# A hybrid decoder trunk on one core: the swap of the rotary halves by transfers inside SBUF in place of copies on ACT

## The chip, the cores and the metric

The kernel runs on one core of a Trainium2 chip. A core has engines that work side by side, each through its own instructions in order: TensorE (PE, matrix products, with its weight loads shown as PEld), VectorE (DVE), ScalarE (ACT), GpSimd (POOL) and SyncE (SP, which here only issues transfers). The transfers are carried by 16 DMA engines. SBUF is the working memory, 128 partitions wide; PSUM has eight banks that take PE's results. The metric is the device time of one execution, in microseconds (us); lower is better.

## The reference

Two layers over 512 tokens of width 1024, all in float32. Each layer adds three sub-layers to x, each between two RMS norms: a mixer, a gated MLP with a causal convolution of width 3, and a gated embedding. The mixer projects once (`z = h @ w_in`) and splits the columns among three kinds of heads: spatial gating, retention (6 heads of 64) and forgetting attention, FoX (6 heads of 64). The change touches only the rotary step ahead of retention:

```
def rotary(t, positions):
    half = t.shape[-1] // 2
    inv_freq = ROPE_BASE ** (-jnp.arange(half, dtype=jnp.float32) / half)
    ang = positions.astype(jnp.float32)[..., None] * inv_freq
    cos = jnp.cos(ang)[:, :, None, :]
    sin = jnp.sin(ang)[:, :, None, :]
    t1, t2 = t[..., :half], t[..., half:]
    return jnp.concatenate([t1 * cos - t2 * sin, t1 * sin + t2 * cos], axis=-1)
...
        rq = rotary(r_q.astype(jnp.float32).reshape(B, S, N_HEADS_RET, HEAD_DIM), positions)
        rk = rotary(r_k.astype(jnp.float32).reshape(B, S, N_HEADS_RET, HEAD_DIM), positions) * (HEAD_DIM ** -0.5)
        rv = r_v.astype(jnp.float32).reshape(B, S, N_HEADS_RET, HEAD_DIM)
        ro = retention_chunkwise(rq, rk, rv)
```

## The kernel before

**Layout.** Queries and keys of retention are held feature-major: a tile `rm` has 128 partitions, two heads of 64 features, and 512 columns, the tokens. Features 0 to 31 of a head are the first half of the rotary pair, 32 to 63 the second, so swapping the halves moves rows of data between partitions: 32 to 0, 0 to 32, 96 to 64 and 64 to 96.

**The projection.** Weights come in float32 and are split into a high and a low part (a cast on ACT, a subtraction on DVE), so that three faster matmuls make one product. `seven` (L869) computes two 128-row projections, gs and us, at once from seven products instead of eight, in the PSUM banks `beta`, `alpha` and `gamma`; its weights (`graw`, then `wg`, `wu`, `wsa`, `wsb`) need sums that two accumulating transfers from POOL and two adds on DVE make. Its first output is complete with DVE's last add to it, its second with a scaled copy on ACT after the last product, `beta<-hh,wu`.

**The rotary step.** `ret_proj(p)` (L1133) calls `seven` for the query and the key of a pair of heads, then for each of the two matrices `m` takes a scratch tile `rr`, fills it with the swapped halves, and on DVE multiplies m by the cosines in place, rr by the sines, and adds. The in-place product overwrites what the swap reads, so it waits for the swap. `rotary_tables` (L617) makes the two tables once, from positions times the constant `invf`. `ret_core(p)` (L1146) then computes retention for the pair: `ips` are the products of keys and queries, `inn` the decayed scores, `kps` and `kt` the transposed keys, `kvps` and `R` the state, `rops` the outputs, `ro` and `og` their norm and gate, `cc` the concatenation.

**The order of the mixer** is a string of steps (L494):

```
STEPS = "u F H f0 g f1 r0 a0 v a1 G L s r1 r2 c0 f2 c1 c2 a2"
```

f0 to f2 project FoX pairs, a0 to a2 are their attention (`sps` scores, `pe` probabilities, `tps` their transposes, copied to `fet`, then `ops`), r0 to r2 are `ret_proj`, c0 to c2 `ret_core`, v and s belong to retention values and spatial gating, G to the gate. After the mixer come the output projection (weights `traw` to `thl`, products `wo` and `ps`), and the gated MLP in 32 blocks.

**What sets the order on the engines.** The body doesn't issue instructions; it records them. `Plan.record` (L170) notes which recorded operations an operation depends on, by the regions that it reads and writes. `Plan.issue` (L252) then deals the operations out: it steps a clock, keeps for each engine the operations whose inputs are ready and whose buffers can be had, takes the first of them in program order, and advances by a table of costs (L209; a transfer issued by SP costs 525 ns there, then waits for the earlier bytes and 2600 ns more). What comes out is a fixed order for each engine, which the engine follows on the chip, waiting at an instruction whose inputs aren't there. SP's order is made in the same way, so a transfer that waits for its source holds back the transfers behind it on SP. Most small tiles, `rm` and `rr` among them, come from one pool of 12 (L565). An operation that takes another engine or another duration can thus move any operation after it.

Since all operations are recorded through a helper, every row of the trace has line 452; rows are told apart by the names of their tiles.

Of the kernel before, what the change touches and what calls it, by code (L numbers as in the profile page):

```python
# [36 lines left out]
P = 128  # L37
# [433 lines left out]
def constants():  # L471
    idx = np.arange(P, dtype=np.float64)
    lg = np.log(1.0 - 2.0 ** (-5.0 - np.arange(6, dtype=np.float64)))
    diff = idx[None, :] - idx[:, None]
    decay = np.where(diff >= 0, np.exp(lg[:, None, None] * np.maximum(diff, 0.0)), 0.0) / 8.0
    qdec = np.exp(lg[:, None] * (idx + 1.0))
    kdec = np.exp(lg[:, None] * (P - 1.0 - idx)) / 8.0
    cd = np.exp(lg * P)
    hf = np.repeat(np.arange(2), 64)
    c = {}  # L480
    c["ident"] = np.eye(P)
    c["decay"] = decay.transpose(1, 0, 2).reshape(P, 6 * P)
    c["qdec"] = np.stack([qdec[2 * p + hf] for p in range(3)], 1).reshape(P, 3 * P)
    c["kdec"] = kdec.T
    c["cd"] = np.stack([cd[2 * p + hf] for p in range(3)], 1)
    c["invf"] = (10000.0 ** (-np.arange(32, dtype=np.float64) / 32))[np.arange(P) % 32][:, None]
    c["cum"] = np.concatenate([(idx[:, None] <= idx[None, :]).astype(np.float64), np.ones((P, P))], 1)
    c["mask"] = np.where(idx[None, :] <= idx[:, None], 0.0, 1e30)
    return {k: np.ascontiguousarray(v.astype(np.float32)) for k, v in c.items()}
# [51 lines left out]
def body(ctx, tc, a, out):  # L541
    nc = tc.nc
    plan = Plan(tc)
    V, A, G, T, SY = (plan.engine(n, e) for n, e in (
        ("DVE", nc.vector), ("ACT", nc.scalar), ("POOL", nc.gpsimd), ("PE", nc.tensor), ("SP", nc.sync)))
# [19 lines left out]
    def wk(name, shape=(P, 512), dt=F32):  # L565
        return kpt(list(shape), dt, tag="wk", name=name, bufs=12)
# [279 lines left out]
    def seven_weights(src, dma=SUMS_BY_DMA):  # L846

        raw = b8("graw", (2048,))
        load(raw, src.rearrange("p s n -> p (s n)"))
        u2, u1, g1, g2 = (raw[:, i * 512:i * 512 + 512] for i in range(4))  # L850
        wg = b8("wg", (2, 1024), F32R)
        split(wg[:, 0, :], wg[:, 1, :], raw[:, 1024:2048])
        wu = [wk("wu", dt=F32R) for _ in range(2)]
        split(wu[0], wu[1], u2)
        if dma:
            G.dma_start(out=u1, in_=src[:, 0, :], accum_op=ALU.add)
            G.dma_start(out=g1, in_=src[:, 1, :], accum_op=ALU.add)
        else:
            for t, by in ((g1, u1), (u1, u2)):
                V.tensor_tensor(out=t, in0=t, in1=by, op=ALU.add)  # L860
        for t, by in ((u2, g1), (g2, u2)):
            V.tensor_tensor(out=t, in0=t, in1=by, op=ALU.add)
        sa = b8("wsa", (2, 1024), F32R)
        split(sa[:, 0, :], sa[:, 1, :], raw[:, 0:1024])
        sb = b8("wsb", (2, 1024), F32R)
        split(sb[:, 0, :], sb[:, 1, :], raw[:, 1024:2048])
        return wg, wu, sa, sb

    def seven(h, ws, gs, us, scale=1.0, between=None):  # L869

        wg, wu, sa, sb = ws
        be, al, ga = (bank(n)[:, 0:256] for n in ("beta", "alpha", "gamma"))
        t1, t2 = slice(0, 256), slice(256, 512)

        def product(ps, w, n, first, last, part=range(4)):
            for k in part:
                ks = slice(k * P, k * P + P)
                mm3(ps, lambda i: w[i][:, ks], lambda i: h.part(n, i, k), first and k == 0, last and k == 3, True)

        def part(t, i):  # L880
            return [t[:, j, i * 512:i * 512 + 512] for j in range(2)]
        product(be, part(wg, 0), "b11", True, False)
        vbe, val, vga = (in_order(t) for t in (be, al, ga))
        g1, g2, u1, u2 = (halves(t[:, ts]) for t in (gs, us) for ts in (t1, t2))
        A.copy(g1, vbe)
        product(al, part(wg, 1), "b21", True, True)
        V.tensor_tensor(out=g1, in0=val, in1=g1, op=ALU.add)
        product(be, part(sa, 0), "h6", False, False)
        A.copy(g2, vbe)
        product(ga, part(sa, 1), "hd", True, False)  # L890
        if scale == 1.0:
            A.copy(u2, vga)
        else:
            A.mul(u2, vga, -scale)
        product(be, part(sb, 0), "h7", False, False)
        V.scalar_tensor_tensor(out=u2, in0=vbe, scalar=-scale, in1=u2, op0=ALU.mult, op1=ALU.subtract if scale == 1.0 else ALU.add)
        product(ga, part(sb, 1), "b22", False, True)
        V.tensor_tensor(out=g2, in0=vga, in1=g2, op=ALU.add)
        rest = between() if between else None
        product(be, wu, "h4", False, True, range(1) if rest else range(4))  # L900
        if rest:
            rest()
            product(be, wu, "h4", False, True, range(1, 4))
        A.mul(u1, vbe, -scale)
# [60 lines left out]
    def mixers(l, hT, uv, ready):  # L965
# [167 lines left out]
        def ret_proj(p):  # L1133
            res = [wk("rm") for _ in range(2)]
            seven(hT, seven_weights(a["w_fm"][l, p]), *res)
            for m in res:
                r = wk("rr")
                for s in (0, 64):
                    A.mul(r[s:s + 32, :], m[s + 32:s + 64, :], -1.0)
                    A.copy(r[s + 32:s + 64, :], m[s:s + 32, :])  # L1140
                V.tensor_tensor(out=m, in0=m, in1=cosT, op=ALU.mult)
                V.tensor_tensor(out=r, in0=r, in1=sinT, op=ALU.mult)
                V.tensor_tensor(out=m, in0=m, in1=r, op=ALU.add)
            return res
# [59 lines left out]
        for step in STEPS.split():  # L1204
            h = int(step[1]) if len(step) > 1 else 0
            if step == "u":
                gating_proj()
                if l == 0:
                    rotary_tables(sinT, cosT)
                    SY.dma_start(out=trig[:, 0, :], in_=sinT)  # L1210
                    SY.dma_start(out=trig[:, 1, :], in_=cosT)
            elif step == "v":
                ret_values()
            elif step == "s":
                gating()
            elif step == "F":
                fox_values()
            elif step == "L":
                A.activation(sg, sg, AF.Silu)
            elif step[0] == "p":  # L1220
                ready[h] = gate_up_weights(l, h)
            elif step[0] == "f":
                fq[h] = fox_proj(h)
            elif step[0] == "r":
                rq[h] = ret_proj(h)
            elif step == "g":
                ret_gates()
            elif step == "H":
                hT.combine()
            elif step == "G":  # L1230
                ret_gate()
            elif step[0] == "a":
                fox_attend(h, fq[h])
            else:
                ret_core(h, *rq[h])
# [322 lines left out]
```

## Time and profile before

| | us |
|---|---|
| median of 3 runs | 1526.82 (1526.79 to 1529.71) |
| the profiled execution | 1528.62 |
| its span, first to last instruction | 1526.9 |
| PE busy | 1496.3 (98%) |
| DVE busy | 1216.7 (80%) |
| ACT busy | 888.9 (58%) |

The profile is of one execution. A row of a group gives the engine, the operation, the tile written and the tiles read, and how often; a row of the timeline has the start and the length in us, and in brackets how long the engine stood idle before it and whose end it was that released it. SPq and POOLq are the issues of transfers, not the transfers. The mean granted clock of TensorE is 0.998. The mixers of the two layers, with the rotary steps, lie around 60 to 215 us and 815 to 990 us of the span.

### The profile page before, as it was taken

The numbers are of one execution on the slowest core, as the hardware profiler recorded it, in microseconds if no ns is written. First come the engines' busy times: TensorE is split into PE (matmuls) and PEld (weight loads), VectorE is DVE, ScalarE is ACT, GpSimd is POOL, SyncE is SP. The second block draws the span as 40 slices with busy tenths as digits, with TensorE's granted clock in tenths as the row PEclk, the third lists the DMA queues.
The fourth block names the chain that finished last, engine by engine and source line by source line (L and its number), as shares of the span: only waits on it lengthen the run. The fifth ranks groups of instructions, "written<-read, shape, count | busy, mean of one in ns | idle before, by whom it ended". The sixth has DMA issues, their size and how long they took to land.

```text
span 1526.9 us, 26942 instructions
## 1 busy us (share of the span) xinstructions
PE 1496.3 (98%) x10554; PEld 1383.6 (91%) x10554; DVE 1216.7 (80%) x2036; ACT 888.9 (58%) x1501; POOL 194.3 (13%) x233
## 2 busy tenths in 40 slices
PE   8999999999999999999999999999999999999997
PEld 6998888899999999998889887799999999999987
DVE  6888969978778777768797779799688778778685
ACT  8557647755555545545575565587655555455462
POOL 1111102111101111100120102121101011011010
PEclk9999999999999999999999999999999999999999
DMA  9445619735646646556573355295545565465541
GB/s 335 88 135 122 209 52 280 189 90 146 173 90 175 150 117 173 146 155 245 190 197 99 92 146 182 68 334 130 146 117 153 163 149 130 123 174 139 212 174 70
DMA packets 87879, 239.02 MB, mean 157 GB/s; under 512 B 10036, under 2 KB 18364, under 8 KB 87752
## 3 DMA queue, kind: packets, MB, share of 16 engines
q1 hardware_dynamic: 64856, 195.81, 37.6%
q0 software_dynamic: 22464, 40.90, 17.0%
q8 instruction: 83, 1.36, 0.4%
q10 hardware_dynamic: 432, 0.59, 0.1%
q14 instruction: 44, 0.36, 0.1%
HBM read 219.94 MB, written 17.33 MB: 155 GB/s over the span
## 4 chain that ended last, share of the span: by engine, by line
PE 74%; DVE 8%; DMA 5%; ACT 5%; issue 5%; POOL 1%; SPq 0%; POOLq 0%; DVEq 0%; ACTq 0%
PE beta L452 20%; PE dn L452 19%; PE ps L452 13%; PE gamma L452 11%; PE alpha L452 5%; DMA graw<-in_w_gu_dram 3%; DMA traw<-in_w_dn_dram 2%; PE wo L452 1%; ACT rr L452 1%; PE hps L452 1%; DVE cv L452 1%; PE tps L452 1%; PE ops L452 1%; ACT junk L452 1%; POOL y L452 1%
## 5 line engine op out<-in xcount | busy, mean ns | idle before, releaser
L452 PE MATMUL dn<-thl,act 128*128 128x512 f32 x1536 | 351.7, 380 | 0.0
L452 PEld LDWEIGHTS dn<-thl,act 128*128 128x128 f32 x1536 | 281.8, 189 | 35.0
L452 POOL DMA_DIRECT2D graw<-in_w_gu_dram x128 | 112.1, 908 | 733.4 <-DVE wg L452 232.0
L452 PE MATMUL ps<-thl,hT 128*128 128x512 f32 (+3 forms) x984 | 198.7, 358 | 2.5 <-ACT hT L452 2.4
L452 PEld LDWEIGHTS ps<-thl,hT 128*128 128x128 f32 x984 | 171.6, 189 | 19.5 <-ACT hT L452 2.9
L452 DVE TENSOR_TENSOR thl<-traw,thl 128x1024 fp32r<-128x1024 f32 (+3 forms) x124 | 141.8, 1152 | 13.4 <-ACT thl L452 13.3
L452 ACT CAST thl<-traw 128x1024 fp32r<-128x1024 f32 (+3 forms) x124 | 121.2, 995 | 21.2 <-PE dn L452 9.2
L452 PEld LDWEIGHTS beta<-hh,wu 128*128 128x128 f32 x936 | 123.2, 191 | 7.2 <-DVE us L452 1.4
L452 PE MATMUL beta<-hh,wu 128*128 128x256 f32 x936 | 126.2, 275 | 1.0 <-DVE us L452 0.9
L452 PE MATMUL beta<-hh,wsa 128*128 128x256 f32 x936 | 120.6, 277 | 6.1 <-ACT gs L452 3.2
L452 PE MATMUL gamma<-hhd,wsa 128*128 128x256 f32 x936 | 120.8, 277 | 0.9 <-ACT wsa L452 0.8
L452 PEld LDWEIGHTS beta<-hh,wsa 128*128 128x128 f32 x936 | 111.4, 192 | 9.2 <-ACT gs L452 4.4
L452 PE MATMUL beta<-hh,wsb 128*128 128x256 f32 x936 | 118.0, 276 | 0.1
L452 DVE TENSOR_TENSOR graw<-graw 128x512 f32<-128x512 f32 x156 | 106.7, 684 | 10.4 <-DMA graw<-in_w_gu_dram 7.9
L452 PEld LDWEIGHTS gamma<-hhd,wsa 128*128 128x128 f32 x936 | 113.1, 194 | 1.3 <-ACT wsa L452 1.0
L452 PEld LDWEIGHTS beta<-hh,wsb 128*128 128x128 f32 x936 | 111.2, 193 | 0.3 <-ACT gs L452 0.3
L452 ACT CAST wsa<-graw 128x1024 fp32r<-128x1024 f32 x78 | 82.0, 1051 | 43.2 <-PE gamma L452 24.7
L452 DVE TENSOR_TENSOR wg<-graw,wg 128x1024 fp32r<-128x1024 f32 x78 | 95.1, 1219 | 13.0 <-ACT wg L452 12.8
L452 DVE TENSOR_TENSOR wsa<-graw,wsa 128x1024 fp32r<-128x1024 f32 x78 | 95.1, 1219 | 10.0 <-ACT wsa L452 9.9
L452 DVE SCALAR_TENSOR_TENSOR cv<-gs,cw,cv 128x511 f32<-128x511 f32 (+1 forms) x128 | 95.0, 743 | 8.5 <-ACT cv L452 8.2
L452 DVE TENSOR_TENSOR wsb<-graw,wsb 128x1024 fp32r<-128x1024 f32 x78 | 95.0, 1218 | 6.6 <-ACT wsb L452 5.9
L452 ACT CAST wg<-graw 128x1024 fp32r<-128x1024 f32 x78 | 82.1, 1053 | 30.5 <-PE gamma L452 13.2
(225 smaller groups left out, 2620.6 us busy)
## 6 DMA issues: line engine op xcount, KB each, us to landing
graw<-in_w_gu_dram SPq DMA_DIRECT2D x128, 512.0 KB
graw<-in_w_gu_dram POOLq DMA_DIRECT2D x128, 256.0 KB, 5.4
traw<-in_w_dn_dram SPq DMA_DIRECT2D x64, 512.0 KB
x<-x SPq DMA_DIRECT2D x40, 512.0 KB
graw<-in_w_fm_dram SPq DMA_DIRECT2D x28, 512.0 KB
traw<-in_w_wo_dram SPq DMA_DIRECT2D x16, 512.0 KB
traw<-in_w_pg_dram SPq DMA_DIRECT2D x16, 512.0 KB
graw<-in_w_fm_dram POOLq DMA_DIRECT2D x28, 256.0 KB, 5.1
```

The costliest lines, as they stand in the source:

```text
L452: made = o[1](*[self.map(v) for v in o[2]], **{k: self.map(v) for k, v in o[3].items()})
```

## The change

```diff
-    c["invf"] = (10000.0 ** (-np.arange(32, dtype=np.float64) / 32))[np.arange(P) % 32][:, None]
+    c["invf"] = (10000.0 ** (-np.arange(32, dtype=np.float64) / 32))[np.arange(P) % 32][:, None] * np.where(np.arange(P) % 64 < 32, -1, 1)[:, None]
...
             for m in res:
                 r = wk("rr")
-                for s in (0, 64):
-                    A.mul(r[s:s + 32, :], m[s + 32:s + 64, :], -1.0)
-                    A.copy(r[s + 32:s + 64, :], m[s:s + 32, :])
+                for s in range(0, P, 32):
+                    SY.dma_start(out=r[s:s + 32, :], in_=m[s ^ 32:(s ^ 32) + 32, :])
                 V.tensor_tensor(out=m, in0=m, in1=cosT, op=ALU.mult)
```

The four copies on ACT that fill `rr` (two of them with a sign) become four transfers from SBUF to SBUF, 32 partitions of 512 floats each, issued by SP. The sign moves into the frequencies: on the partitions of the first half they are negative, so that the sine there is negated and the cosine stays. `ret_proj` runs three times in each of two layers, for two matrices: 12 matrices, 48 copies and 48 transfers. Since the copies leave ACT and the transfers enter SP, the planner deals out a new order on all engines, from the attention a0 of each layer to the first gate and up blocks behind it.

**SP in layer 0, from the weights of the gate projections on.** `graw<-in_w_fm` are weights of projections, `fcb` the broadcasts for attention, `traw<-in_w_wo` the weights of the output projection. Before:

```order
L452 DMA graw<-in_w_fm_dram 128x1024 x6
L452 DMA fcb<-cums_4_880 128x512
L452 DMA fcb<-cums_5_890 128x512
L452 DMA traw<-in_w_wo_dram 128x1024 x8
L452 DMA eraw<-in_w_pe_dram 128x512
```

And now:

```order
L452 DMA graw<-in_w_fm_dram 128x1024 x2
L452 DMA rr<-rm 32x512 x8
L452 DMA graw<-in_w_fm_dram 128x1024 x4
L452 DMA fcb<-cums_4_880 128x512
L452 DMA fcb<-cums_5_890 128x512
L452 DMA rr<-rm 32x512 x8
L452 DMA traw<-in_w_wo_dram 128x1024 x4
L452 DMA rr<-rm 32x512 x8
L452 DMA pr<-in_p_dram 128x2x256 x2
L452 DMA traw<-in_w_wo_dram 128x1024 x4
```

The swaps of r0 stand ahead of four loads, those of r1 ahead of all output weights, those of r2 in the middle of them.

**DVE in layer 0 after r0**, from the last add to its first matrix (`rm<-gamma,rm`) to that matrix's rotary multiplies; `mix_201` holds the cosines, `mix_168` the sines, `ISA pe,nm` and `den` belong to attention a0. Before:

```order
L452 ISA pe,nm<-sps,fcb 128x128
L452 ISA nm 128x1
L452 TENSOR_TENSOR mix_312<-mix_312,mix_1124 128x256
L452 ISA pe,nm<-sps,fcb,nm 128x128
L452 ISA nm 128x1
L452 TENSOR_TENSOR rm<-rm,mix_201 128x512
L452 TENSOR_TENSOR rr<-rr,mix_168 128x512
L452 RECIPROCAL den<-den 128x1 x2
L452 TENSOR_TENSOR rm<-rm,rr 128x512
```

And now:

```order
L452 TENSOR_SCALAR pe<-pe,den 128x128
L452 ISA pe,nm<-sps,fcb,nm 128x128
L452 ISA nm 128x1
L452 COPY fet<-tps 128x128
L452 ISA pe,nm<-sps,fcb 128x128
L452 ISA nm 128x1
L452 ISA pe,nm<-sps,fcb 128x384
L452 ISA nm 128x1
L452 TENSOR_TENSOR rm<-rm,mix_201 128x512
L452 TENSOR_TENSOR rr<-rr,mix_168 128x512
L452 COPY fet<-tps 128x128
L452 TENSOR_TENSOR rm<-rm,rr 128x512
```

From the last add to the first multiply there were ten rows, and now there are twenty; the reciprocals, the scaled probabilities and the first copy of a transposed block come ahead of it.

**DVE in layer 0 after r1 and r2**, again from the last add to the first matrix. `graw<-graw` are sums of weights, `wsa`, `wsb` and `thl` splits. After r1, before:

```order
L452 TENSOR_TENSOR rm<-gamma,rm 128x256
L452 TENSOR_TENSOR wsb<-graw,wsb 128x1024
L452 TENSOR_TENSOR fcb<-fcb,mix_201 128x512
L452 TENSOR_TENSOR graw<-graw 128x512
L452 TENSOR_TENSOR fcb<-fcb,mix_201 128x512
L452 TENSOR_TENSOR rm<-rm,mix_201 128x512
```

After r1, now:

```order
L452 TENSOR_TENSOR rm<-gamma,rm 128x256
L452 TENSOR_TENSOR graw<-graw 128x512 x2
L452 TENSOR_SCALAR kt<-kps,k_kdec 128x3x64 x2
L452 TENSOR_TENSOR wsa<-graw,wsa 128x1024
L452 TENSOR_TENSOR wsb<-graw,wsb 128x1024
L452 TENSOR_TENSOR rm<-rm,mix_201 128x512
```

After r2, now:

```order
L452 TENSOR_TENSOR rm<-gamma,rm 128x256
L452 TENSOR_TENSOR graw<-graw 128x512
L452 TENSOR_TENSOR wsa<-graw,wsa 128x1024
L452 TENSOR_TENSOR wsb<-graw,wsb 128x1024
L452 TENSOR_TENSOR fqk<-alpha,fqk 128x256
L452 TENSOR_TENSOR inn<-ips,mix_168 128x512 x2
L452 TENSOR_TENSOR thl<-traw,thl 128x1024
L452 TENSOR_REDUCE ss_2053<-rsq 128x8
L452 TENSOR_TENSOR thl<-traw,thl 128x1024
L452 TENSOR_TENSOR rm<-rm,mix_201 128x512
```

After r1 two splits stand ahead of the multiply where one stood; after r2 the multiply, which stood behind one score product, the state `R`, one `thl` and `qd`, comes behind a sum, two splits, two score products and two `thl`. On PE the products `ips` on r1's matrices come, in both layers, after 82 or more projection matmuls of 256 columns from r1's last one.

## The prediction

> **What bounds the kernel now.** I read the page's first part, its chain of waits and its traffic.
>
> ```profile
> span 1526.9 us, 26942 instructions
> PE 1496.3 (98%) x10554; PEld 1383.6 (91%) x10554; DVE 1216.7 (80%) x2036; ACT 888.9 (58%) x1501; POOL 194.3 (13%) x233
> PE 74%; DVE 8%; DMA 5%; ACT 5%; issue 5%; POOL 1%; SPq 0%; POOLq 0%; DVEq 0%; ACTq 0%
> ...
> DMA packets 87879, 239.02 MB, mean 157 GB/s; under 512 B 10036, under 2 KB 18364, under 8 KB 87752
> ```
>
> TensorE is busy for 98% of the span; only about 30 us are not its own. A change that leaves its matmuls alone can win at most part of these. Next, the rows of the swapped tile, and the windows of the two stretches that hold all of them (one per layer; the columns after the length are PE, PEld, DVE, ACT, POOL, then the granted clock, DMA share and GB/s).
>
> ```profile
> L452 ACT ACTIVATE rr<-rm x24: 627/630/634, 97.6 to 916.2; 32x512 f32<-32x512 f32 x24
> L452 ACT COPY rr<-rm x24: 615/618/627, 98.2 to 916.9; 32x512 f32<-32x512 f32 x24
> 60.00:215.00 155.00, 152.78 (x1173) 136.43 (x1172) 131.71 (x335) 95.78 (x180) 19.09 (x21) 1.00 0.45 126
> 815.00:990.00 175.00, 169.07 (x1206) 146.84 (x1205) 140.12 (x337) 102.96 (x199) 23.64 (x26) 1.00 0.43 124
> ```
>
> The 48 copies are 24 x 0.630 + 24 x 0.618 = 30.0 us of ACT. But in these stretches PE idles only 155.00 - 152.78 = 2.2 and 175.00 - 169.07 = 5.9 us, and the clock is full: **8.1 us is the most the change can win there**. ACT, at about 60%, is not the bound; DVE, at 80 to 85%, is the fuller helper. Which of those idle times end on the swap? The timelines of layer 0 and layer 1 (idle time before, and its releaser, in brackets):
>
> ```profile
> 104.61 0.61 ACT L452 COPY rr<-rm 32x512 f32<-32x512 f32 x1
> 105.26 0.69 DVE L452 TENSOR_TENSOR rm<-rm,mix 128x512 f32<-128x512 f32 x1 [1.58 <-ACT rr L452]
> 106.47 0.28 DVE L452 COPY fet<-tps 128x128 f32<-128x128 f32 x1
> 106.81 0.33 PE L452 MATMUL tps<-k_ident,pe 128*128 128x128 f32 x1 [1.51 <-DVE fet L452]
> ...
> 852.31 0.69 DVE L452 TENSOR_TENSOR rm<-rm,mix 128x512 f32<-128x512 f32 x1 [1.58 <-ACT rr L452]
> 853.86 0.33 PE L452 MATMUL tps<-k_ident,pe 128*128 128x128 f32 x1 [1.35 <-DVE fet L452]
> 902.66 0.49 PE L452 MATMUL gamma<-hhd,wsa 128*128 128x256 f32 x2 [0.84 <-ACT wsa L452]
> 904.22 1.16 PE L452 MATMUL ips<-rm 64*128 64x128 f32 x16 [0.79 <-DVE rm L452]
> 922.33 0.92 PE L452 MATMUL wo<-thl,cc 128*128 128x512 f32 x3 [0.69 <-ACT thl L452]
> ```
>
> DVE works in order. At 105.26 the rotary multiply has stood 1.58 us for the last copy; the small copy of a transposed attention block behind it, which frees a PSUM bank, comes late, and PE waits 1.51 us for that bank. Layer 1 repeats this (1.35). At 902.66 PE waits for a weight cast that ACT does behind a row of swap copies; at 904.22 for the rotated matrix itself (922.33, a wait on another cast, has other causes beside). Together **1.51 + 1.35 + 0.84 + 0.79 = 4.5 us** of PE idle that trace to the copies.
>
> **What goes.** The copies and these four waits. I count all 4.5 us: in the new order of DVE the first rotary multiply of r0 stands behind ten more rows, most of them attention's, which no longer queue behind it; the casts have no copies ahead on ACT; and between r1's last projection matmul and the first product on r1's matrices PE now has 82 others.
>
> ```profile
> 146.68 1.50 PE L452 MATMUL beta<-hh,wu 128*128 128x256 f32 x12
> 148.02 1.50 PE L452 MATMUL beta<-hT,wg 128*128 128x256 f32 x12
> ```
>
> A dozen takes 148.02 - 146.68 = 1.34 us, so these are over 9 us of cover. The sign costs nothing: it is in a constant, and the sine of a negated angle is the negated sine, the cosine unchanged.
>
> **What comes.** 48 transfers of 32 x 512 floats, 64 KB each, 3.1 MB beside the 239 MB that move now. No SBUF-to-SBUF transfer exists in this trace, so issue and landing are bounded from the nearest rows, SP's and their consumers'.
>
> ```profile
> 73.44 1.77 SPq L452 DMA_DIRECT2D cums<-mix  x6
> 75.32 6.49 SPq L452 DMA_DIRECT2D fcb<-cums  x4
> 81.02 0.80 SPq L452 DMA_DIRECT2D fcb<-cums  x2
> 81.86 2.17 SPq L452 DMA_DIRECT2D traw<-in_w_rv_dram  x4
> 84.07 0.67 SPq L452 DMA_DIRECT2D sguw<-in_sgu_w_dram  x1
> 91.30 0.88 POOL L452 TENSOR_SCALAR_AFFINE_SELECT sguw<-sguw 128x512 f32<-128x512 f32 x1 [14.39 <-DMA sguw<-in_sgu_w_dram]
> ```
>
> *Issue*: 1.77 / 6 = 0.30 to 0.80 / 2 = 0.40 us each, so 1.2 to 1.6 us for a matrix's four; I take 1.6. *Landing, low end*: the first load of a stored row starts at 75.32, after that row's store of 73.44, so a small transfer on a quiet queue lands within 1.9 us. *High end*: the 256 KB issued at 84.07, right behind four weight loads of 384 KB, release POOL at 91.30, 7.2 us later. A swap, small but in a queue with weight loads, I put at 2.5 us where no large load stands ahead, since it is then nearest to the low row.
>
> One matrix then takes 1.6 + 2.5 = 4.1 us (3.5 to 8.8) where four copies took 2.5. For a pair the difference shrinks: the eight copies run in series, 5.0 us, while the transfers of both overlap. Both matrices' first DVE multiply must wait, since it overwrites what the transfers read. Three things decide whether the delay reaches PE:
>
> *The path to the product.* r0's matrices are used tens of us later, r1's over 9 us later, of which the swap, three multiplies and their queue take some 7; a delay of 2 us more is covered, and r2's have f2's projection and output matmuls ahead of them.
>
> *DVE's queue.* Behind a waiting multiply stands everything of DVE, and DVE has no room to recover (two windows of the layer-0 stretch with r1 and r2):
>
> ```profile
> 140.00:150.00 10.00, 10.00 (x91) 9.55 (x88) 9.83 (x16) 7.39 (x13) 0.86 (x1) 1.00 0.57 107
> 150.00:160.00 10.00, 9.91 (x99) 9.29 (x99) 9.89 (x18) 6.91 (x12) 0.00 (x0) 1.00 0.54 167
> ```
>
> The groups of DVE that stand before the multiplies in the new order (busy total and mean ns after the bar):
>
> ```profile
> L452 DVE TENSOR_TENSOR thl<-traw,thl 128x1024 fp32r<-128x1024 f32 (+3 forms) x124 | 141.8, 1152 | 13.4 <-ACT thl L452 13.3
> L452 DVE TENSOR_TENSOR graw<-graw 128x512 f32<-128x512 f32 x156 | 106.7, 684 | 10.4 <-DMA graw<-in_w_gu_dram 7.9
> L452 DVE TENSOR_TENSOR wsa<-graw,wsa 128x1024 fp32r<-128x1024 f32 x78 | 95.1, 1219 | 10.0 <-ACT wsa L452 9.9
> L452 DVE TENSOR_TENSOR wsb<-graw,wsb 128x1024 fp32r<-128x1024 f32 x78 | 95.0, 1218 | 6.6 <-ACT wsb L452 5.9
> ```
>
> Between the last write of r1's first matrix and its multiply the new order puts two adds of weights (2 x 0.68) and two splits (2 x 1.22): 3.8 us of cover against 4.1 needed. For r2 it puts one add, two splits and two output weights: 0.68 + 2.44 + 2 x 1.15 = 5.4 us and smaller rows. So at 2.5 us of landing DVE waits about 0.3 us in r1 and nothing in r2; at 7.2 us it waits 8.8 - 3.8 = 5.0 in r1 and 8.8 - 5.4 = 3.4 in r2. I take 0.5 us per layer on PE: **+1.0 us**.
>
> *SP's queue.* SP now stands until the matrices are ready, and weight loads stand behind it.
>
> ```profile
> 95.24 1.85 SPq L452 DMA_DIRECT2D graw<-in_w_fm_dram  x2
> 121.07 11.27 SPq L452 DMA_DIRECT2D graw<-in_w_fm_dram  x4
> 149.22 0.81 SPq L452 DMA_DIRECT2D traw<-in_w_wo_dram  x2
> 156.73 0.80 SPq L452 DMA_DIRECT2D traw<-in_w_wo_dram  x2
> 169.39 0.81 SPq L452 DMA_DIRECT2D traw<-in_w_wo_dram  x2
> ```
>
> r0's swaps are out by about 102 us; the loads behind them could not go before 121.07 anyway, which is 19 us of cover. r1's swaps, ready from 148, push the output weights of 149.22 back by some 3 us; they are first read over 5 us after they land. Without that cover a load would cost its lateness, up to 3 us. I put 0.
>
> *The rest of the plan.* The planner deals out the same matmuls in another order from the mixers to the first gate and up blocks. A new order has its own small gaps; the stretches' idle time beyond the four waits is 8.1 - 4.5 = 3.6 us, and I let it grow by **1.0** (from 0 to doubling, 3.6).
>
> **Sum**: -4.5 + 1.0 + 1.0 = **-2.5 us**. The profiled execution took 1528.6 us for its span of 1526.9, 1.8 us above the median of the runs, 1526.8. Against its own time that is 1526.1; against the median **1524.3 us**.
>
> **A rule against the change.** The Trainium skill, "DMA: Bandwidth & Descriptors", section "Rules for kernel authors", says that transfers below 64 KB are mostly overhead and that splitting one over disjoint partitions brings nothing because the parts serialize. Four parts at its fixed cost of about 2 us (section "Anatomy of one DMA") would, as an estimate, be 8 us a matrix instead of 4.1. The six stores above speak against serial fixed costs: they were issued in 1.77 us and the first was read back 0.1 us after the last went out.
>
> **The rivals.**
>
> *The plan absorbs it.* The four waits go but gaps of the same size open elsewhere: DVE as full as above gets no work taken away, only ACT does. For it: DVE is the fuller helper. Against it: the four waits are plainly caused by the copies. Time: -4.5 + 4.5, 1526.8.
>
> *Swaps late behind weight loads (slower).* In the new order SP sends r2's swaps behind four output-weight loads of 512 KB, and r1's behind two broadcasts. If a swap lands like the 256 KB at 84.07, DVE stands 5.0 + 3.4 us per layer, with 9.8 of 10 us busy around it, and PE's banks come free late. If half of 2 x 8.4 reaches PE, that is +8.4 - 4.5 + 1.0 = +4.9: 1531.7. It decides once landing exceeds some 5 us. Against it: the output weights go out when buffers free, often long before r2 is ready (169.39 is after it).
>
> The Trainium skill states, in the same page's section "Queues, rings and completion order", that descriptors start in ring order and that a completion lands only after the engine's earlier writes, which is this rival's mechanism; the 7.2 us above agree, though no run here shows it for a swap.
>
> *Nearly all idle time goes.* With 30 us off ACT the remaining small waits on casts shrink too (the 0.69 at 922.33 is the largest of them). Of the 8.1 us some 7 go: 1520.
>
> **How the numbers follow.** This kernel's measurement can tell about 0.2%, 3.05 us, from no change: faster means below 1523.8, slower above 1529.9. Forecast 0.42, of which its own spread of 1521.5 to 1527 puts 0.24 below 1523.8 and 0.18 within. Absorbed 0.16, within. Late swaps 0.28, slower. Nearly all gone 0.14, faster. Faster 0.38, same 0.34, slower 0.28. The range reaches into both outer cases: 1518 to 1533.
>
> **What would show it.** Right: the rows of the swapped tile are gone from ACT, which is some 30 us less busy; PE no longer waits over 1 us for the first attention copies near 106 and 853 us; a swap takes 2 to 3 us from issue to landing. Wrong: DVE's rotary multiplies wait on the transfers for more than 1 us each, with DVE's splits and PE's matmuls of r1, r2 and f2 late behind them; or PE idles over 8 us in the two stretches, or between the output product and the first gate and up blocks, in places that have nothing to do with the swap.

## The result and the profile after

The changed kernel takes 1517.9 us (median of 5 runs, 1515.67 to 1521.04) against 1527.85 for the kernel before, measured beside it: a ratio of 0.9934, 95% interval 0.9914 to 0.9954, so about 10 us faster where 2.5 were forecast, and 0.1 us outside the range of 1518 to 1533. A second measurement gave 0.9936 (0.9921 to 0.9952). The profiled execution of the change took 1515.67 us, 13.0 us less than the 1528.62 of the one before; its page (length, busy times, chain of waits, traffic):

```profile
span 1513.9 us, 26968 instructions
PE 1491.4 (99%) x10554; PEld 1379.6 (91%) x10554; DVE 1217.5 (80%) x2036; ACT 859.1 (57%) x1453; POOL 195.0 (13%) x233
PE 85%; DVE 7%; ACT 3%; issue 2%; DMA 2%; POOL 1%; SPq 0%; DVEq 0%; POOLq 0%; ACTq 0%
...
DMA packets 90184, 242.18 MB, mean 160 GB/s; under 512 B 10804, under 2 KB 19132, under 8 KB 90056
```

ACT is 888.9 - 859.1 = 29.8 us less busy, the 30.0 of the copies, and 3.1 MB more move. But the span got 13.0 us shorter, and PE accounts for all of it: its idle time went from 1526.9 - 1496.3 = 30.6 to 1513.9 - 1491.4 = 22.5 us, 8.1 less, and its busy time, with the same 10554 matmuls, by 4.9. Part of that busy time can be traced. A dozen matmuls of 256 columns reads 1.50 us, right behind a wait often 1.60; with fewer waits there are 14 such longer rows in place of 23, some 0.9 us. Another 1.7 us is one stretch of a halved clock, shown below. The rest, over 2 us, lies in small differences of many rows and was not traced. The swapped tile's row and the two stretches with the mixers:

```profile
L452 SPq DMA_DIRECT2D rr<-rm x48: 507/588/1062, 97.5 to 911.0; - x48
60.00:215.00 155.00, 152.59 (x1161) 135.32 (x1160) 130.42 (x333) 78.98 (x153) 19.56 (x21) 1.00 0.47 136
815.00:990.00 175.00, 173.15 (x1237) 151.70 (x1236) 146.69 (x349) 92.91 (x187) 25.75 (x30) 1.00 0.50 147
```

PE now idles 155.00 - 152.59 = 2.4 and 175.00 - 173.15 = 1.9 us there, 8.1 - 4.3 = 3.8 us less than before. That is near the 2.5 forecast, and it is less than half of the 8.1 us of idle time that went. Where the rest lies is seen in the view that sums PE's waits by the tile waited for (total, times, longest). Before:

```profile
PE beta L452 <- ACT gs L452: 3.2, 5, 1.4
PE tps L452 <- DVE fet L452: 2.9, 2, 1.5
PE beta L452 <- DVE wsa L452: 2.6, 2, 2.2
PE hps L452 <- DVE h L452: 2.5, 5, 0.6
...
PE beta L452 <- DVE us L452: 0.9, 1, 0.9
PE gamma L452 <- ACT wsa L452: 0.8, 1, 0.8
PE ips L452 <- DVE rm L452: 0.8, 1, 0.8
...
PE wo L452 <- ACT thl L452: 0.7, 1, 0.7
PE beta L452 <- DVE wg L452: 0.6, 1, 0.6
```

And after:

```profile
PE hps L452 <- DVE h L452: 3.7, 8, 0.6
...
PE gamma L452 <- ACT us L452: 1.7, 1, 1.7
...
PE rops L452 <- DVE R L452: 1.2, 2, 0.7
PE beta L452 <- ACT gs L452: 0.8, 2, 0.5
...
PE alpha L452 <- ACT hb L452: 0.5, 1, 0.5
```

All rows of this view add up to 21.8 us before and 14.2 after, 7.6 less. The four waits of the forecast (2.9 for `fet`, 0.8 for `wsa` from ACT, 0.8 for `rm`) are all gone: 4.5. New or longer ones, `us`, `R`, `h`, `hb`, take back some 4.3. And some 7.4 went that the forecast had not put down to the swap: 2.6 for a split of weights, 2.4 of the 3.2 for `gs`, and smaller ones. Those two stand in the gate and up blocks of the MLPs, behind the mixers, where the change touches no operation (timeline of before):

```profile
290.73 1.53 PE L452 MATMUL beta<-hh,wsa 128*128 128x256 f32 x10 [2.25 <-DVE wsa L452]
292.06 2.77 PE L452 MATMUL gamma<-hhd,wsa 128*128 128x256 f32 x12
...
410.50 1.60 PE L452 MATMUL beta<-hh,wsa 128*128 128x256 f32 x12 [1.42 <-ACT gs L452]
...
1323.36 1.60 PE L452 MATMUL beta<-hh,wsa 128*128 128x256 f32 x12 [0.70 <-ACT gs L452]
```

The group of these matmuls shows it in one row, 6.1 us of idle time ahead of it before, 0.1 after:

```profile
L452 PE MATMUL beta<-hh,wsa 128*128 128x256 f32 x936 | 120.6, 277 | 6.1 <-ACT gs L452 3.2 <-DVE wsa L452 2.6 <-ACT fqk L452 0.2
```

```profile
L452 PE MATMUL beta<-hh,wsa 128*128 128x256 f32 x936 | 119.7, 276 | 0.1
```

The row at 292.06, behind the longest of these waits, takes 2.77 us where a dozen takes 1.50. The granted clock of TensorE was halved there: it stands at 0.50 for 3.41 us from 291.83 on, which costs 1.7 us. The profile after has no such stretch before the last matmuls of the execution. Nor has a second profile of the kernel before (in the next part), with the same wait of 2.25 us at the same place (the columns are those of the windows above; first profile, then second):

```profile
292.00:295.00 3.00, 3.00 (x16) 3.00 (x15) 3.00 (x5) 1.70 (x4) 0.00 (x0) 0.50 0.99 236
292.00:295.00 3.00, 2.83 (x26) 2.64 (x24) 3.00 (x5) 3.00 (x6) 0.00 (x0) 1.00 0.98 245
```

Sixteen matmuls lie in these 3 us in the one, twenty-six in the other. A wait can thus cost more than its length, and not in every execution.

Where in the program the time went is told by the lengths of four stretches of PE, in two profiles of each kernel. A layer's first stretch runs from its first cumulative-sum product (`cumps`) to the first output product of its MLP (`dn`), the second from there to the last output product.

| us | before | before, second | after | after, second |
|---|---|---|---|---|
| layer 0, mixer to first `dn` | 226.9 | 226.0 | 225.7 | 226.8 |
| layer 0, MLP | 424.2 | 423.3 | 424.2 | 424.7 |
| layer 1, mixer to first `dn` | 236.5 | 236.4 | 229.0 | 229.1 |
| layer 1, MLP | 426.8 | 425.5 | 422.3 | 423.9 |

Layer 1's first stretch won 7.4 us in both pairs, its MLP 1.6 to 4.5, and layer 0 nothing beyond the spread, though each layer has 24 of the 48 transfers.

In the two traces PE's rows agree, by operation, tile name and shape, over the last 3444 of 10554, most of layer 1's MLP among them, but DVE's only over the last 108 and ACT's over the last 83: the new plan mixed casts, splits and gates otherwise through that block too. So the question for the chip was whether the swap or the plan that was dealt with it won the 10 us.

### The profile page after: what moved, and what is told of

It is laid out like the page before. It is cut to its first block, busy times and chain, and to the rows that moved or that the text cites. A ratio compares the mean times of both kernels' runs of the same rounds, so it can differ in the third digit from the quotient of the medians.

```text
span 1513.9 us, 26968 instructions
## 1 busy us (share of the span) xinstructions
PE 1491.4 (99%) x10554; PEld 1379.6 (91%) x10554; DVE 1217.5 (80%) x2036; ACT 859.1 (57%) x1453; POOL 195.0 (13%) x233
## 4 chain that ended last, share of the span: by engine, by line
PE 85%; DVE 7%; ACT 3%; issue 2%; DMA 2%; POOL 1%; SPq 0%; DVEq 0%; POOLq 0%; ACTq 0%
PE beta L452 25%; PE dn L452 22%; PE gamma L452 12%; PE ps L452 12%; PE alpha L452 6%; PE wo L452 1%; DMA graw<-in_w_gu_dram 1%; PE hps L452 1%; PE sps L452 1%; PE ops L452 1%; PE tps L452 1%; ACT junk L452 1%; PE gps L452 1%; DVE x L452 1%; DVE thl L452 1%
## 5 line engine op out<-in xcount | busy, mean ns | idle before, releaser
L452 DVE TENSOR_TENSOR facc<-dn,facc 128x512 f32<-128x512 f32 x112 | 76.6, 685 | 34.6 <-PE dn L452 34.5
L452 ACT CAST wg<-graw 128x1024 fp32r<-128x1024 f32 x78 | 82.2, 1054 | 38.2 <-PE gamma L452 20.2
```

The source lines that it names most:

```text
L452: made = o[1](*[self.map(v) for v in o[2]], **{k: self.map(v) for k, v in o[3].items()})
```

## The experiments

**How far one order can be trusted: the two kernels again.** One more execution of the kernel before (1525.26 us, span 1523.6), and four more of the change, whose ratio of 0.9936 is told above.

> The kernel before once more, for a second profile. The time from the first gate and up product of layer 1 to its last output product was 426.5 us against 421.9 in the changed kernel's profile. If that 4.5 us is the order's, it is there again (425 to 427 us); if it is a hazard of one execution's transfers, it is 422 to 424 us this time.

> The changed kernel once more, timed. Both theories: 1516 to 1521 us, 7 to 11 us under before. A second profile tells whether layer 1's mixer (cumulative-sum product to the first output product of the MLP) takes 229 us again, against 236.5 before, and layer 0's 225.8 against 226.9.

Two executions of one kernel differ by some 3 us of span and 2 of PE's waits (19.6 and 21.8 before; 16.5 and 14.2 after), so only differences of several us in one profile mean anything. In the table above layer 1's first stretch is the same to 0.1 us in both profiles of either kernel, so it is the order's. Over both pairs of profiles the span is 10.0 us shorter, the waits 5.3 and PE's busy time 3.9.

**The order and the swap apart.** First the change's order on every engine, with each transfer carried out as a copy on ACT at that place; then the order of before, with each copy carried out as a transfer.

```diff
                 for s in range(0, P, 32):
                     SY.dma_start(out=r[s:s + 32, :], in_=m[s ^ 32:(s ^ 32) + 32, :])
+                    plan.instead("ACT", nc.scalar.copy, (r[s:s + 32, :], m[s ^ 32:(s ^ 32) + 32, :]), {})
```

> The order of all engines is that of the changed kernel, instruction for instruction, but each transfer is carried out as a copy on ACT, at the place that its issue had in time. Theory 'ACT relieved' (the gain is the 30 us off ACT and what waited behind the copies): the gain goes, 1524 to 1528 us. Theory 'new order' (the gain is that the rotary multiplies now stand behind the attention and weight rows, so nobody waits for the swap, whoever makes it): 1516 to 1521 us.

```diff
                     A.mul(r[s:s + 32, :], m[s + 32:s + 64, :], -1.0)
+                    plan.instead("SP", nc.sync.dma_start, (), dict(out=r[s:s + 32, :], in_=m[s + 32:s + 64, :]))
                     A.copy(r[s + 32:s + 64, :], m[s:s + 32, :])
+                    plan.instead("SP", nc.sync.dma_start, (), dict(out=r[s + 32:s + 64, :], in_=m[s:s + 32, :]))
```

> The order of all engines is that of the kernel before, but each copy is carried out as a transfer issued by SP at the place in time that the copy had. Theory 'ACT relieved': most of the gain is there, 1517 to 1523 us. Theory 'new order': the multiplies stand close behind the swap as before and now wait for issue and landing, some 6 us for a pair against 5 of copies, DVE waits 1 to 3 us more per pair, 1527 to 1535 us.

(`instead` lets the plan be dealt with the recorded operation and its cost, and emits the other one in its place.) Copies in the new order: 1539.94 us, ratio 1.0075 (1.0058 to 1.0091). Transfers in the old order: 1542.65, ratio 1.0082 (1.0062 to 1.0101). Both times lie above every range that either theory had set. Neither part gains alone; each costs some 12 us, and together they gain 10. An order fits the operations that it was dealt for. In the first kernel ACT's queue carries what it was not dealt for, seen in PE's waits and in ACT's timeline ahead of the longest:

```profile
PE beta L458 <- ACT fqk L458: 8.9, 3, 4.3
```

```profile
924.79 1.26 ACT L458 COPY rr<-rm 32x512 f32<-32x512 f32 x2
926.08 1.04 ACT L458 CAST wsa<-graw 128x1024 fp32r<-128x1024 f32 x1
927.15 1.24 ACT L458 COPY rr<-rm 32x512 f32<-32x512 f32 x2
...
930.74 0.37 ACT L458 COPY fqk<-beta 128x256 f32<-128x256 f32 x1
```

The copy that frees PE's bank stands behind the swap copies, and PE waits 4.3 us for it. In the second kernel DVE meets its multiplies with the swaps still under way (DVE's waits, then two places of its timeline and PE's):

```profile
DVE rm L458 <- DMA rr<-rm: 18.0, 9, 5.6
```

```profile
97.83 5.70 SPq L458 DMA_DIRECT2D rr<-rm  x8
103.58 0.69 DVE L458 TENSOR_TENSOR rm<-rm,mix 128x512 f32<-128x512 f32 x1 [2.65 <-DMA rr<-rm]
105.85 0.33 PE L458 MATMUL tps<-k_ident,pe 128*128 128x128 f32 x1 [2.50 <-DVE pe L458]
...
857.07 0.69 DVE L458 TENSOR_TENSOR rm<-rm,mix 128x512 f32<-128x512 f32 x1 [3.29 <-DMA rr<-rm]
859.34 0.47 PE L458 MATMUL tps<-k_ident,pe 128*128 128x128 f32 x1 [3.24 <-DVE pe L458]
```

It is a wait of the same kind as in the kernel before, and longer. There PE waited 1.51 and 1.35 us for the copy `fet`, which stood behind the second matrix's multiply; here it waits 2.50 and 3.24 us one transposition earlier, for the probabilities `pe`, which stand behind the first matrix's. A transfer is not quicker than the copies. What takes most of the wait away in the change, as far as these orders show, is that twenty rows of DVE, not ten, stand ahead of the multiply: PE waits 0.22 us for `pe` in the one profile of the change, 0.79 in the other, both in layer 0. No run varies these rows alone.

**One layer at a time.** Transfers in one layer, copies without the sign in the other; the plan is dealt anew.

```diff
-                    SY.dma_start(out=r[s:s + 32, :], in_=m[s ^ 32:(s ^ 32) + 32, :])
+                    if l == 0:
+                        SY.dma_start(out=r[s:s + 32, :], in_=m[s ^ 32:(s ^ 32) + 32, :])
+                    else:
+                        A.copy(r[s:s + 32, :], m[s ^ 32:(s ^ 32) + 32, :])
```

> Transfers in layer 0's mixer, copies on ACT (all without a sign, which is in the table) in layer 1's; the planner deals out its own order. By the two profiles layer 0 gained 1 us and layer 1 the rest. If the gain belongs to layer 1's transfers: 1525 to 1528 us. If it can come from any new order behind layer 0: anywhere from 1517 to 1530 us, with layer 1's mixer not at 236.5 us.

> Copies in layer 0's mixer, transfers in layer 1's. If the gain belongs to layer 1's transfers and the order they bring: 1517 to 1521 us, layer 1's mixer at 228 to 231 us. If it was luck of one plan: anywhere from 1517 to 1530 us.

Layer 0 alone: 1528.31 us, ratio 0.9998 (0.9984 to 1.0012). Layer 1 alone: 1525.92, ratio 1.0003 (0.9982 to 1.0023). Layer 1's first stretch took 237.5 us with transfers in layer 0 alone, and 233.6 with transfers in layer 1 alone, not the 228 to 231 that were expected of transfers there. Two halves worth nothing each make a whole worth 10 us. A gain that belonged to the transfers would add up; this one doesn't.

**The order dealt again with nothing changed.** The planner adds a time behind each instruction of an engine (131 ns for ACT, 128 for DVE). A few ns more or less there change no operation, but the whole order.

```diff
-    HOP = {"PE": 197, "DVE": 128, "ACT": 131, "POOL": 80, "SP": 0}
+    HOP = {"PE": 197, "DVE": 128, "ACT": 135, "POOL": 80, "SP": 0}
```

The kernel with copies:

> The kernel before with no change to any operation; the planner believes that ACT's results arrive 4 ns later (135 in place of 131), so it deals out another order from layer 0's mixer on. Theory 'a new order is worth up to 10 us either way': 3 to 10 us from before, either sign. Theory 'the swap itself': within 3 us of before, since the copies are still on ACT.

> The kernel before, with its copies on ACT, dealt again with the time behind an ACT instruction altered from 131 to 127 ns: a third draw of the order with copies, beside 1523.9 us (135 ns) and 1528.0 us. Theory 'the transfers win it': 1523 to 1530 us, apart from the band of the draws with transfers. Theory 'the draw of the order wins it': the two bands overlap, and this one may well come out at 1520 us or under.

> As the last, with 4 ns more for DVE's results (132 in place of 128): a second draw of the same. Theory 'order alone': 3 to 10 us from before, either sign. Theory 'the swap itself': within 3 us of before.

> The kernel before, with its copies, dealt again with the time behind a DVE instruction at 124 ns: the partner of the run above. Both theories: 1522 to 1531 us, like the four orders with copies so far (1523.9 to 1528.9).

> The kernel before, with copies, dealt again with the time behind an ACT instruction at 139 ns: the partner of the run above. Its order stands close to the one drawn at 135 ns, so both theories: 1522 to 1527 us, near that one's 1523.9.

The kernel with transfers:

> The changed kernel with one number of the planner altered (the time it adds behind an ACT instruction, 131 to 135 ns), so that the four transfers per matrix stay and the whole order is dealt again. Theory 'the transfers win it': the wait on the ACT copies is gone in every order, so the time stays near the changed kernel's 1518 us (1515 to 1522), and layer 1's stretch from the cumulative sums to the down product stays near 229 us. Theory 'the draw of the order wins it': the time comes out anywhere in the band in which the dealt orders of the kernel with copies lie (1524 to 1528), and layer 1's stretch goes back to 233 us or more.

> The changed kernel dealt again with the same number altered the other way (131 to 127 ns). Same two theories as for 135 ns: 1515 to 1522 us and about 229 us in layer 1's stretch if the transfers win it in whatever order; 1524 us or more and 233 us or more if the order as drawn won it.

> The changed kernel dealt again with the time behind a DVE instruction altered (128 to 132 ns). Same two theories: 1515 to 1522 us if the transfers win it in whatever order; 1524 us or more if the order as drawn won it. This edit moved the kernel with copies by nothing (1528.0 against 1528.0), so what it does here is a second draw of the order alone.

> The changed kernel dealt again with the planner's time behind a DVE instruction at 124 ns (128 before). If the transfers win about 3 us in themselves and the order drawn moves the time by some 7 us either way: anywhere from 1516 to 1531 us, and 3 us less than its partner with copies only on the mean over the pairs. If the transfers win 10 us: 1515 to 1521 us, and 7 us or more below its partner.

> The changed kernel dealt again with the planner's time behind an ACT instruction at 139 ns (131 before); its order differs from the change's on every engine. If the transfers win about 3 us in themselves and the order drawn moves the time by some 7 us either way: 1516 to 1531 us. If the transfers win 10 us in any order: 1515 to 1521 us.

And one pair in which the swap has the price that I read from the traces, 618 ns for a copy, and 625 ns of SP with 1.0 us to the landing for a transfer:

> The kernel before with the copy of 32 partitions priced in the plan as its trace shows: 618 ns on ACT (190 ns and 0.84 ns an element) in place of 588. The order is dealt again. If a truer price is what the order of before lacked: 1520 us or under. If the order is a draw: 1522 to 1531 us, like the other orders with copies.

> The changed kernel with a swap's transfer priced in the plan as the trace of it shows: 625 ns of SP for an issue and 1.0 us from there to the landing, in place of 525 ns and 2.6 us behind a shared transfer rate. The order is dealt again. If a truer price is what an order lacks: 1516 us or under. If the order is a draw: anywhere from 1516 to 1531 us. If the transfers win 10 us in any order: 1515 to 1521 us.

The ratios to the kernel before, with their 95% intervals, and from each profile the sum of PE's waits in us (one order as it was dealt is called a draw):

| number altered | copies | waits | transfers | waits |
|---|---|---|---|---|
| none | 1 | 21.8 | 0.9934 (0.9914 to 0.9954) | 14.2 |
| ACT 135 | 0.9972 (0.9956 to 0.9988) | 21.9 | 0.9931 (0.9914 to 0.9948), the change's order again | 15.0 |
| ACT 127 | 0.9990 (0.9979 to 1.0000) | 23.8 | 1.0028 (1.0011 to 1.0045) | 23.9 |
| ACT 139 | 0.9974 (0.9961 to 0.9986) | 22.0 | 0.9938 (0.9919 to 0.9956) | 13.1 |
| DVE 132 | 1.0000 (0.9985 to 1.0015) | 23.5 | 0.9973 (0.9961 to 0.9986) | 17.5 |
| DVE 124 | 1.0050 (1.0033 to 1.0066) | 28.7 | 0.9971 (0.9960 to 0.9983) | 20.2 |
| the swap's price | 0.9955 (0.9931 to 0.9979) | 17.8 | 1.0052 (1.0033 to 1.0071) | 27.3 |

With ACT at 135 the kernel with transfers got the change's order on every compute engine, so that row repeats it and is no new draw. The other draws with transfers run from 1519.4 to 1534.6 us, those with copies from 1522.6 to 1534.2. With the priced pair left out, draws that differ by a number without meaning spread over 10 us with copies and 14 with transfers, as much as the change moved. The theory that the transfers win 10 us in any order is gone, since four of these draws lie at some 1524 us or above. Two draws came out above the ranges set for either theory, the copies with DVE at 124 (1534.2 us) and the priced transfers (1534.6), and DVE at 132 did not move the kernel with copies at all, where 3 to 10 us had been expected of a new order. The change drew one of the two best orders seen.

What is the swap worth by itself? Over the five pairs in which both kernels have a draw with the same number (none, ACT 127 and 139, DVE 132 and 124) the differences of the ratios (for the first, the mean of the change's two measurements) are -0.0065, +0.0038, -0.0036, -0.0027 and -0.0079: a mean of -0.0034, some -5 us, with a 95% interval of about -14 to +3.5 us. The 4.5 us of the four waits lie well within it, and so does nothing; the pair with altered prices, +0.0097, would bring the mean to -2 us, and without the first pair, whose size was the question, the other four have a mean of some -4. Between 0 and -5 these draws can't decide.

The sum of PE's waits follows the length closely: over the 20 profiles of this study a straight line, span = 1492.5 + 1.55 x waits, leaves 1.7 us (one standard deviation), 3.1 at most. A us of waits that the view shows thus goes with 1.55 us of span, and the halved clock accounts for nearly all of the rest. In 13 of the 20 profiles the clock falls to 0.50 ahead of the end, one to four times, for 3.41 us or twice that: 1.7 us lost in the kernel before, 5.1 in the draw of transfers with ACT at 127, 8.5 in the priced one, 6.8 and 10.2 in the two kernels of the exchange, none in the change's three profiles (the repeat of its order included). PE had stood idle for 1.5 to 3.1 us of the 3.41 ahead of each. All seven waits of over 2.6 us in the 20 profiles have such a stretch within them or beginning less than 1 us behind; of the 20 between 2.0 and 2.6 us eleven have one, so a wait of that length may or may not halve the clock. Taken off the spans, these losses leave 1500.3 + 1.06 x waits. The clocks of all runs agree: 0.999 in all nine of the change, 0.992 to 0.996 in those of the exchange.

**What makes an order with transfers bad** shows in part in the two slow draws. PE's waits with ACT at 127:

```profile
PE tps L452 <- DVE pe L452: 4.3, 5, 3.2
PE beta L452 <- DVE wsa L452: 2.6, 2, 2.3
PE cps L452 <- DVE ro L452: 2.5, 2, 1.9
...
PE beta L452 <- ACT gs L452: 2.1, 6, 0.4
PE ips L452 <- DVE rm L452: 1.7, 1, 1.7
```

The first attention transposes wait again, 3.19 us at 106.74 behind a DVE that stood 1.61 us for r0's swap, and so does the product on r2's matrices, at 179.13 in layer 0, though no swap is on ACT. In the draw with a swap's price at 1.0 us the plan believed the transfers to be early and put the multiplies early (DVE's and PE's rows, and SP's issue):

```profile
97.51 5.74 SPq L456 DMA_DIRECT2D rr<-rm  x8
104.12 0.69 DVE L456 TENSOR_TENSOR rm<-rm,mix 128x512 f32<-128x512 f32 x1 [2.80 <-DMA rr<-rm]
106.56 0.30 PE L456 MATMUL tps<-k_ident,pe 128*128 128x128 f32 x1 [2.52 <-DVE pe L456]
...
862.92 0.69 DVE L456 TENSOR_TENSOR rm<-rm,mix 128x512 f32<-128x512 f32 x1 [2.53 <-DMA rr<-rm]
```

DVE waited 6.9 us for transfers there, in four places, and PE behind it. My price was wrong: I had taken the time at which the last packets of a swap ended for its landing, and DVE is released later, 1.4 to 4.2 us behind the fourth issue. The original price, 525 ns an issue and 2.6 us behind the bytes ahead, was nearer to the truth. How much of this draw's 1534.6 us is due to the price, one draw can't show.

No version among these beat the change beyond its uncertainty: 1517.7 us is the same order, 1519.4 another.

## Why the prediction was wrong

**What goes** (-4.5) came true row by row: no wait on `fet` near 106 and 853 us, none for the cast at 902 or the rotated matrix at 904, and 29.8 us less of ACT. It is true of the order that was drawn; in the draw with ACT at 127 like waits were back.

**What comes**: the issue was mis-sized. It is 0.588 us in the median, not 0.40, so a matrix's four take 2.4 to 2.5 us, not 1.6. The landing, where DVE stood waiting for it in the runs, came between 1.4 and 4.2 us behind the fourth issue (2.5 was taken). From the first issue to the multiply that is 4.3 to 6.7 us a matrix; 4.1 was forecast, in a range of 3.5 to 8.8. The Trainium skill, "DMA: Bandwidth & Descriptors", section "Anatomy of one DMA", gives about 2 us fixed for one transfer, there on the path of transfers issued by GpSimd; by it four serial ones would be an estimated 8 us. The runs, on SP, stay below that sum with 4.3 to 6.7.

**DVE's queue** (+1.0) cost PE less than that, and elsewhere. In the first profile the single wait of the change's DVE for a swap was in r0, not in r1:

```profile
97.52 5.03 SPq L452 DMA_DIRECT2D rr<-rm  x8
103.37 0.69 DVE L452 TENSOR_TENSOR rm<-rm,mix 128x512 f32<-128x512 f32 x1 [0.68 <-DMA rr<-rm]
...
148.60 4.96 SPq L452 DMA_DIRECT2D rr<-rm  x8
153.65 1.98 SPq L452 DMA_DIRECT2D traw<-in_w_wo_dram  x4
154.32 0.69 DVE L452 TENSOR_TENSOR rm<-rm,mix 128x512 f32<-128x512 f32 x1
```

In r1 the multiply starts 5.7 us after the first issue and shows no wait: the matrix had its cover. In the second profile DVE waited in four places, 2.0 us together, three of them in r0; PE's 0.79 us for `pe`, at 108.23, is the one wait of PE seen behind them. **SP's queue** (0) held too: the output weights went out at 153.65 right behind the swaps, and PE's waits after have none on `thl`.

**The rest of the plan** (+1.0, from 0 to 3.6) is the step that failed. It let the new order only add gaps, and only in the two stretches with the mixers. Measured in the first pair of profiles, the new order took away some 7.4 us of waits that the forecast had not put down to the swap, most of them in the gate and up blocks behind, and gave back 4.3; PE's busy time fell by 4.9 besides. Over both pairs the span is 10.0 us shorter, 4.5 of it the four waits, so the new order brought some -5.5 us where +2.0 stood in the sum for it and DVE's queue. Two premises of the prediction led there. "8.1 us is the most the change can win there" was true of the stretches, where 3.8 were won, but the sum then went on as if it bounded the kernel; the first gate and up blocks, which the planner also deals out anew, lie outside the windows, with the 2.25 us wait at 290.73 among them. And "only about 30 us are not its own" counted PE's busy time as fixed, though the same 10554 matmuls took 4.9 us less, 1.7 of it by the clock. The re-dealt orders give the size that the term needed: some 7 us to either side. That the change drew a good one is luck.

**The rivals.** "The plan absorbs it" fell. "Nearly all idle time goes" came nearest in time, for another reason than it gave: idle time outside the stretches, and a shorter busy time. Inside them 3.8 us went, not 7. "Swaps late" named the real danger, though not its condition: it is not a landing past 5 us but the DVE rows that the plan puts between. With the old order's few rows it cost 18.0 us of DVE's time, with a landing as usual. Loads ahead of a swap show at r0 alone (last section).

## What to carry to other kernels

Where a planner deals fixed orders, an edit is two edits: the operation, and a new draw of the whole order. Deal both kernels again with a number that means nothing before reading a gain of under 1% as the operation's, and give the draw a term of its own in a forecast, for the whole program and with both signs. Swapping an operation inside an order made for another one tests neither: here either half cost 12 us.

When a small transfer takes the place of copies, count the rows that stand between it and its in-place reader on that engine; the price in the planner should be the time at which the reader is released, not that at which the bytes have moved (argued from the 6.9 us that DVE waited in the draw with 1.0 us; its cost in time is not shown).

Where matmuls fill the time, look at the granted clock behind each long wait of PE: here a wait of some 2 us could cost 1.7 us more.

## What was not expected of the hardware

A transfer of 64 KB between partitions of SBUF occupies SP for 0.588 us in the median (507 to 1062 ns), where the rows of before gave 0.30 to 0.40 for its other small ones: eight take 5.0 us of SP.

The landing of the same four transfers, counted from the end of the fourth issue to the multiply that waited, was 2.8 to 4.2 us in r0 and 1.4 to 2.4 in r1 and r2. The packets of the change's profile point to a cause: those of the first four end 1.6 us (layer 0) and 2.5 us (layer 1) behind the fourth issue in r0, and 1.1 us in r1 and r2. SP had issued two weight loads of 512 KB 2.3 and 3.6 us ahead of r0's first swap, and their packets moved until 101.2 and 845.4 us, when the swap's had just begun (100.4 and 844.8). That these loads hold r0's swaps back was not tried by a run.

A wait of PE of 1.75 to 2.6 us, or a few shorter ones close together, was followed in some executions by 3.41 us or 6.83 us of TensorE at half its clock, and in others not.
